# A decoder layer step on one core: one array for x's two parts, three blocks in one first stage, and 512-column matmuls in six index query blocks

## The chip, the cores and the metric

The kernel runs on one core of a Trainium2 chip. The metric is the device time of one execution, in microseconds. Five engines run their own instruction streams and meet at semaphores: TensorE (PE in the profile, with its weight loads as PEld), VectorE (DVE), ScalarE (ACT), GpSimd (POOL) and SyncE (SP), which here issues DMA transfers. Matmul results land in PSUM, everything else lives in SBUF.

## The reference

The reference is one inference step of one decoder layer, in float32, for a prompt of 256 tokens and for 8 requests with 8 new tokens and 2048 cached tokens each. Together these are 320 token columns (`NT`): 256 of the prompt, then 64 of the samples. A prompt query keeps 64 keys, so the first 64 prompt tokens (`SKIP = 64`) keep all they have and need no index query. One input projection makes all heads:

```
z = jnp.einsum('btd,dn->btn', h, w)          # d = 2048
aq, ak, av, ag, iq, ik, iw, bq, bf, bi, bg, mq, mg = jnp.split(z, cuts, axis=-1)
iq = _rope(iq.reshape(n_b, n_t, H_IDX, D_IDX), pos)
sc = jnp.einsum('bth,bthl->btl', iw, jax.nn.relu(dots))   # dots = iq . ik
_, sel = lax.top_k(sc, n_sel)                # keys that each query attends to
```

`aq`, `ak`, `av` are queries, keys and values of a sparse attention with 8 heads of 128; `iq` (16 heads of 64), `ik` and `iw` make the index scores that select the keys. A gated linear recurrence (`bq`, `bf`, `bi`), a cross-attention into memory tokens, gates, an output projection and a layer norm follow. The selection depends on order among scores, so the products are made with nearly full float32 precision.

## The kernel before

All large products use a rounded float32 type (`F32R`) that PE streams at one column per cycle. To keep precision, each operand is split in a high part (a cast) and a low part (the operand less its high part), and three products are summed: weight high times x high, weight high times x low, weight low times x high.

x is held transposed, 16 slices of 128 rows and 320 columns: `xh` and `xl` are two arrays of `[128, 16, 320]`. A block of the projection is 128 output columns: its weights are the stationary operand, 16 slices K of 128x128, and the moving operand is x. So a full block is 16 x 3 matmuls of 320 columns, and an index query block (`iq`, eight of them) 16 x 3 of 256 columns, because it leaves out the first 64 tokens. The sum of a block stands in a PSUM bank of the tag `pj`, of which there are two. Other PSUM tags are `mA`, `mB` (two banks each), `va` and `kv`.

For each block SP loads weights (`wr`), ACT casts them to `wh`, DVE (later in the program DVE or POOL) subtracts to `wl`, in pieces of 512 columns; there are four buffers of `wh` and of `wl`. When a block is done, its `ev_...` function takes it from PSUM: for `iq`, DVE shuffles and multiplies with the rotary tables straight from PSUM, and POOL multiplies and adds.

The order of all instructions is written out when the program is built. A planner (`Plan`) keeps an estimated time for each engine and a ready time for each tile; the loop at the end issues the next piece of matmul work when its operands are ready by that plan, and lets generators in a background list put small jobs on DVE, ACT and POOL between. `wspec` is the list of weight pieces in the order in which PE takes them; `half` counts them, and some thresholds (which engine subtracts, when page loads begin) are numbers of such pieces. On the chip the order is fixed, and only semaphores wait.

The list starts with the index keys (`ikw`, 80 columns: 64 of the key, 16 of the weights) and the query block `iq0`, interleaved two slices at a time; then `iq1` to `iq7`, then the eight `aq` blocks, then the rest (`PROJECTIONS`). The first pieces have loads of their own: x in pairs of slices (`in_xT`, the first two pairs on ACT's queue), the index key weights (`in_wik`) and iq0's weights (`in_wt`) in four parts each. Before that, PE runs 32 matmuls on a zeroed tile (`kv<-t`, bfloat16, 256 columns).

Once index keys and queries exist, `idx_load`, `key_scores` and others compute scores and selection in the background; cached pages stream through (`pg` tiles), and PE alternates between projection blocks and page work. Names of buffers carry a number that tells one use of a tag from the next.

Of the kernel before, what the change touches and what calls it, by code (L numbers as in the profile page):

```python
# [28 lines left out]
SKIP = 64  # L29
HALF = 1032  # L30
PROJECTIONS = ["ikw", "iq", "aq", "ak", "av", "b0", "b1", "g0", "b2", "g1", "b3", "mem", "mq", "g3", "g2"]
# [26 lines left out]
class Plan:  # L58
# [61 lines left out]
    def dma(self, q, out, in_):  # L120
# [15 lines left out]
        self.t["DMA"] = end = max(self.t["DMA"], t, 0.9) + nbytes / (380e3 if t > 7 else 270e3)  # L136
# [91 lines left out]
def hymba_step(ctx: ExitStack, tc: tile.TileContext, I, O):  # L228
# [85 lines left out]
    xh = const([128, 16, NT], "xh", F32R)  # L314
    xl = const([128, 16, NT], "xl", F32R)
# [18 lines left out]
    plan.split |= {early.tensor.name, stacked.tensor.name}  # L334
    plan.skip |= {xh.tensor.name, xl.tensor.name, avS.tensor.name}
# [27 lines left out]
    def ev_iq(i):  # L363
        def f(ps):
            if i == 0:
                st["q"] = new([128, 8, NS], "pg")
            c, s = (t[:, SKIP:] for t in tabi)
            sh, x = T(256), T(256)
            DVE.stream_shuffle(sh, ps[:, SKIP:], sh_idx)
            DVE.tensor_mul(x, ps[:, SKIP:], c)  # L370
            POOL.tensor_mul(sh, sh, s)
            POOL.tensor_add(st["q"][:, i, :], x[:, 256 - SKIP:], sh[:, 256 - SKIP:])
            IQ[i] = T(256 - SKIP)
            POOL.tensor_add(IQ[i], x[:, 0:256 - SKIP], sh[:, 0:256 - SKIP])
            free(x, sh)
            if i == 7:
                free(*tabi)
            done.add(("iq", i))
        return f

# [143 lines left out]
    def add_block(kind, i):  # L524
        nk = 2 if (kind, i) in (("ikw", 0), ("iq", 0)) else 8
        if kind == "ikw":
            add_T(I["wik"], ev_ikw, 80, nk)
# [3 lines left out]
        else:  # L531
            base, ev = {"iq": (32, ev_iq), "aq": (0, ev_aq), "ak": (8, ev_ak), "av": (16, ev_av), "mq": (56, ev_mq),
                        "bf": (44, None), "bq": (40, None), "bi": (48, None), "g": (24, None)}[kind]
            if kind == "g":
                add_T(wt[24 + i if i < 8 else 44 + i if i < 12 else 48 + i], ev_gate(i, i % 4 == 3))
            else:
                add_T(wt[base + i], ev(i) if ev else ev_b((kind, i)), nk=nk, skip=SKIP if kind == "iq" else 0)

    for name in PROJECTIONS:
        if name[0] == "b":  # L540
# [3 lines left out]
        else:  # L544
            todo = [(name, i) for i in range({"ikw": 1, "mem": 1, "mq": 4}.get(name, 8))]
        for kind, i in todo:
            add_block(kind, i)
    wspec[0:16] = [wspec[8 * (i % 2) + i // 2] for i in range(16)]
# [61 lines left out]
    def prep(i, j):  # L610
# [29 lines left out]
        if i < 52:  # L640
# [1002 lines left out]
    def half_ready(i, q):  # L1643
        s = wspec[i]
        if i not in WH:
            return False
        p = part_of(i, q)
# [609 lines left out]
```

## Time and profile before

| | |
|---|---|
| median of 3 runs | 858.19 us (858.04 to 858.48) |
| profiled execution | 858.96 us, of which the span of instructions is 857.2 us |
| granted clock of PE over the span | 0.997 |
| matmuls, as the profile counts them | 6904 |
| data moved by DMA | 266.49 MB, 311 GB/s in the mean |

A line of a group has the engine, the operation, the tile that it writes and those that it reads, partitions by columns, the count, the busy time and the mean time of one. A matmul is shown with the time from its start until its modelled end (0.28 us for 256 columns), but the next one starts long before that, so what a matmul costs is the time from start to start. The profile puts nearly all instructions on one helper line (L156), so tiles and times tell them apart, not lines.

### The profile page before, as it was taken

How to read it: one execution, taken by the hardware profiler on the slowest of the kernel's cores; microseconds unless marked ns; L12 is line 12 of the kernel's file. 1: busy time of each engine (PE TensorE's matmuls, PEld its weight loads, DVE VectorE, ACT ScalarE, POOL GpSimd, SP SyncE). 2: the span in 40 equal slices, each digit the busy share in tenths (PEclk: the TensorE clock that was granted, in tenths of full speed). 3: DMA queues.
4: the chain of work that ended last, by engine and by line, in shares of the span. 5: the costliest groups of instructions: out<-in, count | busy, mean ns of one | idle time of the engine just before them, and what ended most of it. 6: DMA issues, size and time to landing. Idle time of an engine off the chain costs nothing.

```text
span 857.2 us, 19206 instructions
## 1 busy us (share of the span) xinstructions
PE 846.6 (99%) x6904; PEld 719.7 (84%) x6906; DVE 552.4 (64%) x1103; ACT 425.8 (50%) x915; POOL 310.5 (36%) x323
## 2 busy tenths in 40 slices
PE   9999999999999999999999999999999999999996
PEld 8999988889989888878878888777887889888885
DVE  6698999564987985743574547557545343954655
ACT  6555666544445435444454554555445353744432
POOL 0576653256634461220132214333311100724424
PEclk9999999999999999999999999999999999999998
DMA  8765555799999999999999999999999988856633
GB/s 312 217 184 171 177 151 177 277 377 383 411 378 383 357 335 354 382 379 402 386 325 412 408 349 400 403 393 375 345 410 401 337 337 283 281 172 199 194 97 122
DMA packets 84368, 266.49 MB, mean 311 GB/s; under 512 B 10609, under 2 KB 21810, under 8 KB 83634
## 3 DMA queue, kind: packets, MB, share of 16 engines
q1 hardware_dynamic: 82962, 262.52, 83.9%
q0 software_dynamic: 1024, 2.10, 0.8%
q8 instruction: 54, 0.88, 0.4%
q10 hardware_dynamic: 288, 0.66, 0.3%
q14 instruction: 40, 0.33, 0.1%
HBM read 256.50 MB, written 8.73 MB: 309 GB/s over the span
## 4 chain that ended last, share of the span: by engine, by line
PE 98%; DVE 1%; ACT 0%; issue 0%; DVEq 0%
PE pj L156 56%; PE mB L156 12%; PE va L156 10%; PE mA L156 10%; PE kv L156 8%; PE kv L1926 1%; DVE pg L156 0%; DVE t L156 0%; DVE cat L156 0%; DVE wl L156 0%; ACT t L156 0%; ACT wh L156 0%; DVE s L156 0%; DVEq L156 0%; DVEq L2243 0%
## 5 line engine op out<-in xcount | busy, mean ns | idle before, releaser
L156 ACT CAST wh<-wr 128x512 fp32r<-128x512 f32 x338 | 207.3, 619 | 244.2 <-PE pj L156 182.3
L156 PE MATMUL pj<-xh,wh 128*128 128x320 f32 (+1 forms) x1008 | 318.9, 316 | 0.0
L156 PE MATMUL pj<-xh,wl 128*128 128x320 f32 (+1 forms) x1008 | 308.6, 306 | 0.1
L156 PE MATMUL pj<-xl,wh 128*128 128x320 f32 (+1 forms) x1008 | 308.3, 306 | 0.0
L156 DVE TENSOR_TENSOR wl<-wr,wh 128x512 fp32r<-128x512 f32 x236 | 179.5, 767 | 194.4 <-ACT wh L156 177.8
L156 POOL TENSOR_TENSOR wl<-wr,wh 128x512 fp32r<-128x512 f32 x102 | 136.9, 1347 | 243.0 <-ACT wh L156 198.3
L156 PEld LDWEIGHTS pj<-xh,wh 128*128 128x128 f32 x1008 | 189.6, 188 | 18.3 <-issue 15.0
L156 PEld LDWEIGHTS pj<-xl,wh 128*128 128x128 f32 x1008 | 189.8, 188 | 1.3
L156 PEld LDWEIGHTS pj<-xh,wl 128*128 128x128 f32 x1008 | 189.5, 188 | 0.3 <-DVE wl L156 0.3
L156 POOL TENSOR_TENSOR t<-t,t 128x256 f32<-128x256 f32 (+3 forms) x53 | 46.2, 871 | 118.9 <-ACT t L156 54.4
L156 PE MATMUL kv<-pg,qpad 128*32 128x256 f32 (+1 forms) x916 | 59.2, 380 | 0.0
L156 PE MATMUL va<-pg,PT 128*32 128x512 f32 x456 | 58.4, 595 | 0.0
L156 PEld LDWEIGHTS kv<-pg,qpad 128*32 128x32 f32 (+1 forms) x916 | 31.6, 110 | 21.0 <-issue 1.9
L156 PEld LDWEIGHTS va<-pg,PT 128*32 128x32 f32 x456 | 14.6, 109 | 30.4 <-issue 28.1
L156 DVE MAX8 PT<-PT 128x8 f32<-128x1032 f32 x32 | 39.5, 1233 | 0.5
L156 DVE MATCH_REPLACE8 PT<-PT 128x1032 f32<-128x1032 f32 x32 | 39.0, 1218 | 0.0
L156 POOL DMA_INDIRECT S<-in_ci,row x24 | 25.5, 1062 | 25.3 <-DVE row L156 17.3
L156 PE MATMUL mB<-t,wh 128*128 128x256 f32 x128 | 24.4, 289 | 0.0
L156 POOL TENSOR_TENSOR t<-t,tabm 128x320 f32<-128x320 f32 x16 | 14.1, 880 | 28.4 <-DVE t L156 27.8
L156 POOL TENSOR_TENSOR bp<-t,bp 128x128 f32<-128x128 f32 (+1 forms) x17 | 10.5, 620 | 37.0 <-ACT bp L156 37.0
L156 ACT ACTIVATE S<-kv 128x512 f32<-128x512 f32 x16 | 9.6, 597 | 27.7 <-PE kv L156 27.7
L156 PEld LDWEIGHTS mB<-t,wh 128*128 128x128 f32 x128 | 20.7, 191 | 1.2
(384 smaller groups left out, 1339.1 us busy)
## 6 DMA issues: line engine op xcount, KB each, us to landing
wr<-in_wt SPq DMA_DIRECT2D x126, 512.0 KB
pg<-in_ck SPq DMA_DIRECT2D x114, 512.0 KB
pg<-in_cv SPq DMA_DIRECT2D x114, 512.0 KB
wr<-in_wo SPq DMA_DIRECT2D x36, 512.0 KB
wr<-in_wm SPq DMA_DIRECT2D x16, 512.0 KB
S<-in_ck SPq DMA_DIRECT2D x14, 512.0 KB
S<-in_cv SPq DMA_DIRECT2D x14, 512.0 KB
pg<-in_cXV SPq DMA_DIRECT2D x8, 512.0 KB
```

Source lines behind the costliest of these rows:

```text
L156: res = f(*a, **k)
L1926: nc.tensor.matmul(warm_ps, warm[:, 0:128], warm, start=True, stop=True)
```

## The change

1. `xh` and `xl` become two halves of one array `xhl` of `[128, 16, 2, 320]`: for each slice the high part stands beside the low part.
2. The index keys, `iq0` and `iq1` become one first stage of ten pieces (`FIRST = 10`): four of one slice, six of two. A piece is one transfer of x and all three blocks' weights of that slice, from an array `in_first` laid out on the host, 656 columns a slice (320 of x, 80 + 128 + 128 of weights). All ten go through SP's queue. For each piece ACT casts x, ACT (DVE for the first two) casts the weights, and DVE makes both low parts. PE takes all three blocks in turn, into banks of `va`, `mA` and `pj`; the sums are the same.
3. The other six index query blocks are mixed with the `aq` blocks: aq0, iq2, iq3, iq4, aq1, iq5, iq6, aq2, iq7, aq3 to aq7.
4. In these six, the weight's high part is multiplied with x's high and low part in one matmul of 512 columns, into the two halves of a bank; the weight's low part times x's high part adds 256 columns to the first half. ACT copies the second half out and DVE adds the first half, before shuffle and product, which now read SBUF.
5. 18 warm-up matmuls instead of 32; some small loads and the iota on POOL are issued earlier; the thresholds that count pieces go down by eight, as the list has eight fewer pieces ahead of them; the planner's early transfer rate goes from 270 to 350 KB per us.

```diff
-PROJECTIONS = ["ikw", "iq", "aq", "ak", "av", "b0", ...
+PROJECTIONS = ["first", "queries", "ak", "av", "b0", ...
+FIRST = 10
...
-    xh = const([128, 16, NT], "xh", F32R)
-    xl = const([128, 16, NT], "xl", F32R)
+    xhl = const([128, 16, 2, NT], "xhl", F32R)
+    xh, xl = xhl[:, :, 0, :], xhl[:, :, 1, :]
...
+            x = T(256)
+            if i > 1:
+                ACT.copy(x, ps[:, 1, :])
+            plan.pinned.add(ps.tensor.name)
+            bg.insert(0, [rotate_query(i, ps, x), None])
...
+    def rotate_query(i, ps, x):
+        c, s = (t[:, SKIP:] for t in tabi)
+        sh = T(256)
+        if i > 1:
+            yield need(x, ps=0)
+            DVE.tensor_add(x, x, ps[:, 0, :])
+        y = x if i > 1 else ps[:, SKIP:]
+        DVE.stream_shuffle(sh, y, sh_idx)
+        DVE.tensor_mul(x, y, c)
+        plan.pinned.discard(ps.tensor.name)
...
-        if i < 52:
+        if i < 44:
             DVE.tensor_sub(lo[:, 0:w], raw, hi[:, 0:w].bitcast(F32))
...
+    def first_quantum(i):
+        s = wspec[i]
+        if i == 0:
+            s["ps"] = [PS([128, NT], which) for which in ("va", "mA", "pj")]
+        else:
+            s["ps"] = wspec[i - 1]["ps"]
+        h3, l3 = s["w"]
+        for w, x in ((h3, xh), (h3, xl), (l3, xh)):
+            for ps, c, x0 in zip(s["ps"], firsts, (0, SKIP, SKIP)):
+                for j, K in enumerate(s["ks"]):
+                    PE.matmul(ps[0:c.stop - c.start, x0:], w[:, j, c], x[:, K, x0:],
+                              start=K == 0 and w is h3 and x is xh, stop=K == 15 and w is l3)
...
             for j, K in ks:
+                if x0:
+                    PE.matmul(both, h3[:, j, :], xhl[:, K, :, x0:], start=K == 0, stop=K == 15, skip_group_check=True)
+                    PE.matmul(ps, l3[:, j, :], xh[:, K, x0:], start=False, stop=K == 15, skip_group_check=True)
+                    continue
...
+    def prep_first(a):
+        s = wspec[a]
+        t, ks = s["ks"][0] // 2, slice(s["ks"][0], s["ks"][-1] + 1)
+        raw = raws[t][:, first_cols(a, NT + WIDE)].rearrange("p (j c) -> p j c", c=NT + WIDE)
+        hi, lo = (x[t][:, first_cols(a, WIDE)].rearrange("p (j c) -> p j c", c=WIDE) for x in (his, los))
+        ACT.copy(xh[:, ks], raw[:, :, 0:NT])
+        (ACT.copy if a > 1 else DVE.tensor_copy)(hi, raw[:, :, NT:])
+        DVE.tensor_sub(xl[:, ks], raw[:, :, 0:NT], xh[:, ks].bitcast(F32))
+        DVE.tensor_sub(lo, raw[:, :, NT:], hi.bitcast(F32))
...
-    for _ in range(32):
+    for _ in range(18):
         nc.tensor.matmul(warm_ps, warm[:, 0:128], warm, start=True, stop=True)
```

The order moves at the start and in the query blocks. First PE's first real matmuls, right behind the warm-ups. `PT`, `qpad` and `bp` hold high parts of weights there, `cat` and `pg` low parts; `va` is the sum of the index keys, `mA` of iq0, `pj` of iq0 before and iq1 now. Before:

```order
L156 MATMUL va_186<-xh,PT_88 80x320
L156 MATMUL va_186<-xh,cat_4_84 80x320
L156 MATMUL va_186<-xh,PT_88 80x320
L156 MATMUL va_186<-xh,cat_4_84 80x320
L156 MATMUL va_186<-xl,PT_88 80x320 x2
L156 MATMUL pj_193<-xh,qpad_89 128x256
L156 MATMUL pj_193<-xh,pg_90 128x256
L156 MATMUL pj_193<-xh,qpad_89 128x256
L156 MATMUL pj_193<-xh,pg_90 128x256
L156 MATMUL pj_193<-xl,qpad_89 128x256 x2
```

and in the change:

```order
L157 MATMUL va_184<-xhl,PT_93 80x320
L157 MATMUL mA_185<-xhl,PT_93 128x256
L157 MATMUL pj_186<-xhl,PT_93 128x256
L157 MATMUL va_184<-xhl,PT_93 80x320
L157 MATMUL mA_185<-xhl,PT_93 128x256
L157 MATMUL pj_186<-xhl,PT_93 128x256
L157 MATMUL va_184<-xhl,cat_4_83 80x320
L157 MATMUL mA_185<-xhl,cat_4_83 128x256
L157 MATMUL pj_186<-xhl,cat_4_83 128x256
```

Before, two slices at a time go through two blocks; now one slice at a time goes through three blocks, first with the high parts of x and weights, then with x's low part, then with the weights' low part.

Second, PE at the first index scores: `mA<-t,t` are products of index keys and a rotated query. Before, in block iq3:

```order
L156 MATMUL mA_559<-t_325,t_85 128x64
L156 MATMUL mA_561<-ident,t_325 128x16 x2
L156 MATMUL pj_509<-xh,wh_479 128x256
L156 MATMUL pj_509<-xl,wh_479 128x256
L156 MATMUL pj_509<-xh,wl_480 128x256
```

and in the change, right after block aq0, in block iq2:

```order
L157 MATMUL mA_477<-t_356,t_84 128x64
L157 MATMUL mB_479<-ident,t_356 128x16 x2
L157 MATMUL pj_519<-xhl,wh_395 128x512
L157 MATMUL pj_519<-xhl,wl_396 128x256
L157 MATMUL pj_519<-xhl,wh_395 128x512
L157 MATMUL pj_519<-xhl,wl_396 128x256
L157 MATMUL pj_519<-xhl,wh_395 128x512
L157 MATMUL pj_519<-xhl,wl_396 128x256
L157 MATMUL pj_519<-xhl,wh_395 128x512
L157 MATMUL pj_519<-xhl,wl_396 128x256
L157 MATMUL mA_532<-t_355,t_385 128x128
L157 MATMUL mA_533<-t_355,t_385 128x128
```

Twelve matmuls of 256 columns lie between the first two rows and the scores before, of which three are shown; now four of 512 and four of 256 do.

Third, DVE in the same place. Before:

```order
L156 TENSOR_TENSOR wl_533<-wr_404,wh_532 128x512
L156 TENSOR_TENSOR wl_549<-wr_404,wh_548 128x512
L156 CAST row_552<-rows 128x2
L156 TENSOR_TENSOR t_492<-mA_559,csm 128x4x8 x2
L156 TENSOR_TENSOR t_493<-mA_559,csm 128x4x8 x2
L156 TENSOR_SCALAR cat_3_83<-mA_561 128x32
```

and in the change:

```order
L157 TENSOR_TENSOR wl_445<-wr_323,wh_444 128x512
L157 CAST row_448<-rows 128x2
L157 TENSOR_TENSOR wl_471<-wr_323,wh_470 128x512
L157 TENSOR_TENSOR t_414<-mA_477,csm 128x4x8 x2
L157 TENSOR_TENSOR t_415<-mA_477,csm 128x4x8 x2
L157 TENSOR_SCALAR cat_3_82<-mB_479 128x32
L157 STREAM_SHUFFLE t_508<-pj_363 128x320
L157 TENSOR_TENSOR t_509<-pj_363,tabm 128x320
```

A weight subtraction stands right ahead of the five small jobs in both; after them, the change takes block aq0 (`pj_363`) from its bank.

More of the change, by code (lines that the diff above doesn't have):

```diff
@@ L1646, in half_ready @@
             return False
+        if s["kind"] == "first":
+            return max(plan.avail(x) for x in s["w"]) <= plan.now
         p = part_of(i, q)
@@ L1650, in half_ready @@
         if s["kind"] == "T":
-            return s["k0"] or q or sum(e[0] is not ev_ikw for e in pending) < 2 and plan.slot_free("pj", 2) <= plan.now
+            return s["k0"] or q or sum(e[0] not in other_bank for e in pending) < 2 \
+                and plan.slot_free("pj", 2) <= plan.now
         if s["kind"] == "mem":
@@ L1900, in load_first @@
[L1900 to L1920 removed]
+    WIDE = 80 + 128 + 128
@@ new lines, in hymba_step @@
+    firsts = (slice(0, 80), slice(80, 208), slice(208, WIDE))
+    bps = [new([128, 1024], "bp", F32R) for _ in range(2)]
+    raws = [early[:, 0:1312], early[:, 1312:2624]] + [new([128, 1312], tag) for tag in ("S", "S", "S", "pg", "pg", "pg")]
+    tiles = [new([128, 2320], "PT", F32R), new([128, 2048], "qpad", F32R)], [stacked, new([128, 2048], "pg", F32R)]
+    his, los = ([t[:, 2 * WIDE * i:2 * WIDE * i + 2 * WIDE] for t in ts for i in range(3)] for ts in tiles)
+    his += [t[:, 0:2 * WIDE] for t in bps]
@@ new lines, in hymba_step, with first_cols, load_first @@
+    spare_lo = new([128, 2048], "pg", F32R)
+    los += [spare_lo[:, 2 * WIDE * i:2 * WIDE * i + 2 * WIDE] for i in range(2)]
+    plan.split.update(t.tensor.name for t in raws + his + los)
+    def first_cols(a, w):
+        ks = wspec[a]["ks"]
+        return slice(w * (ks[0] % 2), w * (ks[0] % 2 + len(ks)))
+    def load_first(a):
+        t, c = wspec[a]["ks"][0] // 2, first_cols(a, NT + WIDE)
+        SP.dma_start(raws[t][:, c], I["first"][t][:, c])
+    def prep_first(a):
[7 more added lines that the diff above has]
+        DVE.tensor_sub(lo, raw[:, :, NT:], hi.bitcast(F32))
+        s["w"], WR[a], WH[a], WL[a] = (hi, lo), None, [hi], [lo]
@@ L1955, in setup @@
             SP.dma_start(t, I[n])
+        yield from wait("first")
+        st["qpad"] = new([128, 8, 8, 32], "qpad")
         yield need(pidx)
-        pf, dcol = const([128, 64], "rows"), T8()
-        POOL.iota(dcol[:, 0:1], pattern=[[0, 1]], base=0, channel_multiplier=1,
-                  allow_small_or_imprecise_dtypes=True)
-        DVE.tensor_scalar(dcol[64:128, 0:1], dcol[64:128, 0:1], -64.0, None, op0=OP.add)
+        pf = const([128, 64], "rows")
         DVE.tensor_scalar(pf, pidx, 64.0, dcol[:, 0:1], op0=OP.mult, op1=OP.add)
@@ L2064, in loads @@
             n, b = divmod(npg, 2)
-            if half > 46 and n < len(punits) and page_tag(n) and plan.t["DMA"] < plan.now + 4:
+            if half > 38 and n < len(punits) and page_tag(n) and plan.t["DMA"] < plan.now + 4:
                 load_pages(n, b)
@@ L2075, in loads @@
                 continue
-            if half > 40 and plan.t["SP"] <= plan.now:
+            if half > 32 and plan.t["SP"] <= plan.now:
                 numbers_ahead()
```

134 lines of the change are left out of this document (53 added, 81 removed).

## The prediction

> **What bounds the kernel now.** I read the engine totals first, then the chain of work that ended last, then what TensorE (PE) waited for.
>
> ```profile
> PE 846.6 (99%) x6904; PEld 719.7 (84%) x6906; DVE 552.4 (64%) x1103; ACT 425.8 (50%) x915; POOL 310.5 (36%) x323
> PE 98%; DVE 1%; ACT 0%; issue 0%; DVEq 0%
> PE kv L1926 <- DVE t L156: 1.1, 1, 1.1
> PE mA L156 <- DVE cat L156: 0.9, 1, 0.9
> PE mB L156 <- DVE t L156: 0.3, 1, 0.3
> ```
>
> PE is busy 99% of the span and is 98% of the chain. Its three waits (total, times, longest, in us) add up to 2.3 us. So the time is PE's work, plus its start, plus a tail; what the other engines do counts only where they make PE wait. A change is worth what it takes off PE's own stream. Two stretches could break this reading (columns: length, then busy time and count of PE, PEld, DVE, ACT, POOL, then clock, DMA share, GB/s):
>
> ```profile
> 40.00:60.00 20.00, 19.88 (x167) 19.16 (x167) 19.77 (x45) 10.81 (x22) 13.24 (x15) 1.00 0.54 158
> 350.00:690.00 340.00, 339.61 (x3069) 273.25 (x3070) 188.70 (x404) 164.04 (x378) 87.49 (x104) 1.00 1.00 382
> ```
>
> From 40 to 60 us, in the query blocks, VectorE (DVE) is as full as PE. From 350 to 690 us the DMA engines are full beside a full PE. Both return below as rivals.
>
> **The start.** Pieces of the chain (start, length, what, count):
>
> ```profile
> 1.07 5.81 PE kv L1926 x32
> 6.88 0.87 PE va L156 x6
> 10.23 0.88 PE va L156 x6
> 19.07 15.12 PE pj L156 x126
> 120.25 4.39 PE pj L156 x30
> ```
>
> Then the same start on the timeline, the warm-ups in two windows, and the DMA rate microsecond by microsecond:
>
> ```profile
> 4.61 0.46 ACT L156 CAST PT<-S 128x320 fp32r<-128x320 f32 x1 [1.67 <-DMA S<-in_wik]
> 4.97 0.72 ACT L156 CAST xh<-pg 128x640 fp32r<-128x640 f32 x1
> 5.10 0.49 DVE L156 TENSOR_TENSOR cat<-S,PT 128x320 fp32r<-128x320 f32 x1 [4.08 <-ACT PT L156]
> 5.73 0.83 DVE L156 TENSOR_TENSOR xl<-pg,xh 128x640 fp32r<-128x640 f32 x1
> 6.64 0.39 PE L156 MATMUL va<-xh,PT 128*80 128x320 f32 x1
> 1.10:5.00 3.90, 3.90 (x19) 0.00 (x0) 0.00 (x0) 0.00 (x0) 1.00 0.81 227
> 5.20:6.60 1.40, 1.40 (x13) 0.00 (x0) 0.00 (x0) 0.00 (x0) 1.00 1.04 372
> 1.00:2.00 1.00, 0.93 (x5) 0.67 (x6) 0.01 (x1) 0.34 (x1) 0.94 (x5) 1.00 0.61 31
> 2.00:3.00 1.00, 1.00 (x7) 0.67 (x6) 0.00 (x0) 0.94 (x1) 0.00 (x0) 1.00 0.48 119
> 3.00:4.00 1.00, 1.00 (x6) 0.70 (x5) 0.00 (x0) 0.00 (x0) 0.00 (x0) 1.00 1.06 382
> ```
>
> The first operands are cast by 5.7 us, but the first real matmul starts at 6.64 us, when the 32 warm-ups are through: the warm-ups end that wait, not the data. A warm-up takes some 0.21 us in the first window (19 in 3.90 us) and 0.11 us in the second, so the array speeds up near 5.1 us, although the clock column says 1.00 throughout.
>
> **Part 1, shorter start.** The 126 matmuls of the row at 19.07 take 15.12/126 = 0.120 us each (256 columns); the row of 30 gives 4.39/30 = 0.146 us (320 columns). Six of the 126 end block iq0 and 48 are iq1, so before, the index keys, iq0 and iq1 are done at 19.07 + 54 x 0.120 = 25.55 us. The change does just this work in its first stage. Eighteen warm-ups at 0.21 us, the first of them at 1.07 us, end at about 4.9 us. The work is 48 x 0.146 + 96 x 0.120 = 18.53 us, so it would end at 23.43 us without a wait. Waits it will have: the first piece is 128 x 656 x 4 B = 336 KB, and the last three rows above sum to 532 KB by 4.0 us, so its bytes are in near 3.5 us. How long after that the cast can begin: the two first casts now stand at 4.61 and 4.97 us, so I bound it by 4.1 and 4.9 us and take 4.4. Then DVE does three jobs for each of the first two K slices (a 336-column cast that no row shows, bounded by 0.2 and 0.5 us and taken as the 0.49 of the subtraction of 320), two for the next two slices, all about 0.5 us: its ten jobs end at 9.4 us. PE needs 0.146 + 2 x 0.120 = 0.386 us per third of a slice; following the two rows of jobs against each other it finishes the fourth slice at 10.1 us instead of 9.53. From there a pair costs DVE 0.83 + 0.87 and PE 2.32 us, so PE leads. The stage ends near 24.0 us: **gain 1.55 us** (1.05 with the data at 4.9 us, 2.1 with no wait).
>
> **Part 2, the wide matmuls.** In six index blocks of 16 slices, two 256-column matmuls become one of 512.
>
> ```profile
> 760.02 0.39 PE L156 MATMUL mB<-wh,xh 128*128 128x512 f32 x1
> 760.25 0.39 PE L156 MATMUL mB<-wh,xl 128*128 128x512 f32 x1
> 760.47 0.39 PE L156 MATMUL mB<-wl,xh 128*128 128x512 f32 x1
> 760.70 0.39 PE L156 MATMUL pj<-wh,qpad 128*128 128x512 f32 x1
> ```
>
> From start to start three take 0.68 us, 0.227 each, against 2 x 0.120 = 0.240. The columns are the same; only the 0.013 us per instruction falls away: 96 x 0.013 = **1.25 us**. No row has a moving operand in two stretches 64 columns apart, as here; bounds are 0 (it pays as two) and 1.25, and I take the second, since the operand is otherwise that of these rows. The Trainium skill (TensorE: Matmul & The Clock Gate, "Wait — 56ns, not 53.3ns?") gives a fixed cost of about 2.5 ns per warm matmul; by that the saving would be 96 x 0.0025, an estimate of 0.24 us. The rows above show 13 ns, and they decide.
>
> **Part 3, the wait of 0.9 us** on DVE:
>
> ```profile
> 34.95 1.63 PE pj L156 x12
> 35.80 1.10 DVE L156 TENSOR_TENSOR wl<-wr,wh 128x512 fp32r<-128x512 f32 x1 [1.78 <-ACT wh L156]
> 36.90 0.47 DVE L156 TENSOR_TENSOR t<-mA,csm 128x32 f32<-128x32 f32 x4
> 37.29 0.17 DVE L156 TENSOR_SCALAR cat<-mA 128x32 f32<-128x32 f32 x1
> 37.51 0.93 PE mA L156 x8
> ```
>
> PE ran out of its 12 matmuls at 36.59 us; DVE had still to finish a weight subtraction and five small jobs. In the change this place follows block aq0: PE is there at 24.0 + 48 x 0.146 + 0.6 + 4 x (0.227 + 0.120) = 33.0 us. The subtraction ahead of the small jobs needs a cast whose buffer falls free at aq0's end (31.0 us): 0.6 for the cast, 0.7 for the subtraction, 0.64 for the small jobs, 32.95 us. So the wait is met almost exactly: **gain 0.8 us** (bounds 0 and 0.94).
>
> **Part 4, what is added.** Each wide block has two halves to add.
>
> ```profile
> L156 ACT COPY t<-mB 128x256 f32<-128x256 f32 x11 | 3.7, 375 | 3.2 <-PE mB L156 1.8 <-DVE t L156 1.4
> 26.79 0.45 DVE L156 STREAM_SHUFFLE t<-pj 128x256 f32<-128x256 f32 x1
> 27.13 0.41 DVE L156 TENSOR_TENSOR t<-pj,t 128x256 f32<-128x256 f32 x1
> ```
>
> That is 6 x 0.375 us on ScalarE (ACT) and 6 x 0.41 us on DVE. The two PSUM banks hide it: a bank was free after shuffle and product (0.86 us of work), now after copy and sum (0.79), and PE asks for it again a whole block later, 16 x 0.347 = 5.55 us at least. Mixing main query blocks (48 x 0.146 = 7.0 us) among them stretches DVE's work over more PE time. Moved with the blocks are their loads on SP, the threshold for DVE's subtractions and the page loads' thresholds, each shifted by the eight entries that the list lost, so they stand at the same block as before; the indirect gathers on POOL stay behind the same setup. For waits that the new order makes I allow 0.4 us, with bounds 0 and 2.0, about what the waits of the whole kernel are now without the first.
>
> **Sum.** -1.55 - 1.25 - 0.8 + 0.4 = -3.2 us. The profiled execution took 858.96 us (span 857.2), so 855.8 for it; it lies 0.77 over the median of the runs, 858.19, which gives **855.0 us**.
>
> **Rivals.** (1) The wide form pays as two: no gain in part 2, 856.2 us. For it: no row has the shape; against it: the rows at 760 us.
> (2) PE idles between the last warm-up and the first operands, and the array falls back to the slow rate. The first 19 warm-ups needed 4.0 us to leave it; a second such time at half rate costs 2.0 us: 857.0 us. Against it: the gap is at most 0.5 us. The Trainium skill (same page, "Part 1: The HAM clock gate") has the rate set by activity in a free-running window of about 3.4 us; by that rule 18 warm-ups suffice or fail by where the window lies, and no run here shows where.
> (3) The DMA engines bind from 150 to 690 us, and PE waits there for what it won: 858.2 us. For it: the share of 1.00. Against it: none of PE's waits names a DMA.
> (4) Slower: in the query blocks DVE is the bound, and the bank of each wide block comes free late because copy and sum queue behind weight subtractions. With the 0.9 us of part 3 at each of six blocks, 6 x 0.94 = 5.6 us: 855.0 - 0.4 + 5.6 = 860.2 us. It turns the result from 0.53 us per block on (3.2/6). For it: 19.77 of 20 us on DVE. Against it: that stretch loses PE hardly anything today, and it gets looser.
>
> **How the numbers follow.** Forecast 0.61, rivals 0.07, 0.10, 0.10 and 0.12. About 0.2% (1.7 us) is what a measurement can tell. Forecast and (1) lie below 856.5, (2) mostly above: faster 0.70. (2) and (3) are the same: 0.18. (4) is slower: 0.12. Low end: gains 2.1 + 1.25 + 0.94 and no new wait, 853.9, less 0.9 for waits I don't see: 853.0. High end 858.4, which takes in (3). The likeliest case's own range is 853.5 to 856.4.
>
> **What would show it.** First real matmul near 5.0 us and the first stage done near 24 us; a wide and a narrow matmul together 0.347 us; no wait of 0.9 us on DVE before 40 us; PE waits under 1.5 us in all after the start. Wrong it is if the wide form shows 0.24 us, if the matmuls after 5 us run at 0.21 us, or if PE waits for DVE or ACT at the wide blocks.

## The result, and the profile after

The changed kernel is slower. It takes 865.97 us (median of 4 runs, 865.27 to 866.34) against 858.12 us (857.86 to 858.48) for the kernel before, measured in turn: a ratio of 1.0089, 95% interval 1.0077 to 1.0101, or 7.85 us between the medians. The forecast was 855.0 us.

The page of the changed kernel, its engine totals and its chain of work:

```profile
PE 849.5 (98%) x6793; PEld 715.2 (83%) x6796; DVE 557.2 (64%) x1111; ACT 424.6 (49%) x915; POOL 322.8 (37%) x327
PE 95%; DVE 2%; DMA 2%; ACT 1%; issue 0%; POOL 0%; DVEq 0%; SPq 0%; ACTq 0%; POOLq 0%
```

PE's waits in it (total, times, longest, in us):

```profile
PE kv L157 <- DMA pg<-in_ck: 3.0, 2, 2.3
PE pj L157 <- DVE t L157: 1.6, 1, 1.6
PE kv L1963 <- DVE t L157: 1.1, 1, 1.1
```

PE is no longer 98% of the chain but 95%, and a DMA stands in it with 2%. The wait of 0.9 us on "DVE cat" is gone, as forecast. Two new waits have come: 3.0 us for pages of cached keys (`pg<-in_ck`), and 1.6 us on DVE.

The start ended when it was foreseen. The timeline has the first real matmuls, the end of the first stage (the first matmul of aq0 reads `wh`), and five slices of a wide block:

```profile
4.74 0.62 PE L157 MATMUL va<-xhl,PT 128*80 128x320 f32 x1
5.16 0.41 PE L157 MATMUL mA<-xhl,PT 128*128 128x256 f32 x1
5.37 0.42 PE L157 MATMUL pj<-xhl,PT 128*128 128x256 f32 x1
...
6.36 0.28 PE L157 MATMUL mA<-xhl,cat 128*128 128x256 f32 x1
6.47 0.28 PE L157 MATMUL pj<-xhl,cat 128*128 128x256 f32 x1
...
23.80 0.46 PE L157 MATMUL pj<-xhl,wh 128*128 128x320 f32 x2
...
35.97 0.39 PE L157 MATMUL pj<-xhl,wh 128*128 128x512 f32 x1
36.20 0.29 PE L157 MATMUL pj<-xhl,wl 128*128 128x256 f32 x1
...
37.73 0.40 PE L157 MATMUL pj<-xhl,wh 128*128 128x512 f32 x1
```

The first real matmul starts at 4.74 us (forecast "near 5.0"), the first stage ends at 23.80 ("near 24"). A wide and a narrow matmul together take (37.73 - 35.97)/5 = 0.352 us, against 3 x 0.120 before: 8 ns saved a slice, not 13, so 96 x 8 ns = 0.77 us. One sign of a wrong forecast did come: the first matmuls behind 5 us are slow. From `mA` to `pj` it takes 5.37 - 5.16 = 0.21 us, and 6.47 - 6.36 = 0.11 us a little later. Against the later pace, the matmuls from 4.74 to 6.2 us lose about 0.7 us, and the stage ended on time nevertheless.

What was won is lost later. The chain near the first page products and near 208 us (start, length, what, count), then the rows of the timeline in which PE waits there; the bracket has the wait:

```profile
143.45 0.59 ACT cat L157
144.04 0.49 ACT pg L157
...
145.05 0.68 DVE cat L157
...
145.77 0.70 DVE cat L157
146.49 0.33 SPq L157
...
147.02 6.66 DMA pg<-in_ck
...
198.57 3.66 PE kv L157 x64
202.23 0.08 SPq L157
...
202.51 7.94 DMA pg<-in_ck
```

```profile
150.80 2.35 PE L157 MATMUL kv<-pg,qpad 128*32 128x256 f32 x36
153.82 1.92 PE L157 MATMUL kv<-pg,qpad 128*32 128x256 f32 x28 [0.66 <-DMA pg<-in_ck]
...
210.58 0.41 PE L157 MATMUL kv<-pg,qpad 128*32 128x256 f32 x2 [2.31 <-DMA pg<-in_ck]
```

Two windows around the second wait, and one microsecond inside the second (length, then busy time and count of PE, PEld, DVE, ACT, POOL, then clock, DMA share, GB/s):

```profile
200.00:210.00 10.00, 8.27 (x77) 6.13 (x68) 3.55 (x6) 4.20 (x7) 2.56 (x2) 1.00 0.86 314
210.00:220.00 10.00, 7.82 (x61) 5.02 (x62) 4.01 (x10) 0.25 (x1) 2.68 (x4) 0.83 1.01 404
212.00:213.00 1.00, 1.00 (x16) 0.69 (x12) 0.00 (x0) 0.00 (x0) 0.00 (x0) 0.50 1.03 418
```

Near 150 us, index work on ACT and DVE, which reads a buffer of the tag `pg`, holds it until 146.5 us. Only then can SP issue the page's load. It lands at 153.7 us, and PE, which began on that group of pages at 150.8 us, goes on at 153.82. This costs PE a wait of 0.7 us.

Near 208 us the wait is 2.3 us, and what held the load is another thing: the chain goes back from it to PE's own page products, which end at 202.23 us, and not to index work. Behind this wait the granted clock falls. It is 0.50 from 211 to 214 us and 0.83 in the mean from 210 to 220 us, which is 10 x 0.17 x 2 = 3.4 us at half speed. By the Trainium skill (TensorE: Matmul & The Clock Gate, "Part 1: The HAM clock gate") the array falls to half speed after an idle window of about 3.4 us, and comes back after a busy one of about 3.4 us. The length of the stretch agrees with the second figure; the idle time ahead of it, 2.3 us in one piece, is shorter than the first.

Where the 7.0 us between the two profiled executions lie is seen by the same matmul in both: the first product of page values (`va<-pg,PT`) starts at 367.02 us before and at 371.60 after; the first matmul of the output projection at 731.79 and 736.63; the last matmul at 848.92 and 855.94. So 4.6 us are lost by 367 us, on top of what was won at the start, 0.3 more until 731 us, and 2.2 us in the output projection.

### The profile page after: what moved, and what is told of

Its sections match the earlier page's. It is cut to its first block, busy times and chain, and to the rows that moved or that the text cites. A ratio compares the mean times of both kernels' runs of the same rounds, so it can differ in the third digit from the quotient of the medians.

```text
span 864.2 us, 18969 instructions
## 1 busy us (share of the span) xinstructions
PE 849.5 (98%) x6793; PEld 715.2 (83%) x6796; DVE 557.2 (64%) x1111; ACT 424.6 (49%) x915; POOL 322.8 (37%) x327
## 3 DMA queue, kind: packets, MB, share of 16 engines
q0 software_dynamic: 1024, 2.10, 0.8%
## 4 chain that ended last, share of the span: by engine, by line
PE 95%; DVE 2%; DMA 2%; ACT 1%; issue 0%; POOL 0%; DVEq 0%; SPq 0%; ACTq 0%; POOLq 0%
PE pj L157 54%; PE mB L157 12%; PE va L157 10%; PE mA L157 10%; PE kv L157 8%; DMA pg<-in_ck 2%; PE kv L1963 0%; DVE t L157 0%; DVE cat L157 0%; DVE pg L157 0%; DVE wl L157 0%; DVE bp L157 0%; POOL wl L157 0%; ACT t L157 0%; ACT wh L157 0%
## 5 line engine op out<-in xcount | busy, mean ns | idle before, releaser
L157 PE MATMUL pj<-xhl,wh 128*128 128x320 f32 (+1 forms) x1888 | 440.3, 319 | 1.6 <-DVE t L157 1.6
L157 PEld LDWEIGHTS pj<-xhl,wh 128*128 128x128 f32 x1888 | 316.4, 188 | 25.2 <-issue 12.9
L157 PE MATMUL pj<-xhl,wl 128*128 128x320 f32 (+1 forms) x992 | 304.9, 307 | 0.4 <-DVE wl L157 0.3
L157 DVE TENSOR_TENSOR wl<-wr,wh 128x512 fp32r<-128x512 f32 x226 | 172.8, 773 | 183.4 <-ACT wh L157 167.4
L157 POOL TENSOR_TENSOR wl<-wr,wh 128x512 fp32r<-128x512 f32 x108 | 147.6, 1372 | 247.8 <-ACT wh L157 220.8
L157 PEld LDWEIGHTS pj<-xhl,wl 128*128 128x128 f32 x992 | 186.4, 188 | 1.1 <-DVE wl L157 1.0
L157 PE MATMUL mB<-wh,xhl 128*128 128x512 f32 x108 | 34.0, 396 | 0.0
L157 PE MATMUL mA<-wh,xhl 128*128 128x512 f32 x96 | 30.1, 394 | 0.0
L157 PEld LDWEIGHTS mB<-wh,xhl 128*128 128x128 f32 x108 | 20.3, 188 | 4.7
L157 DVE TENSOR_TENSOR cat<-S,cat 64x512 fp32r<-64x512 f32 x24 | 17.4, 724 | 9.2 <-ACT cat L157 8.6
```

The costliest lines, as they stand in the source:

```text
L157: res = f(*a, **k)
```

## The experiments

Times are medians, with the ratio to the kernel before, run in turn on the same chip, and its 95% interval. "The list" is the fixed order on PE that the planner writes; "planned" is the planner's own estimate of a time, which stands in its `Plan` while the program is built and is here a thing under test, not a measure. Edits are shown abridged. The groups ran on different chips, so kernels of different groups are compared by their ratios.

**First: is it the pages, and what slows the output projection?** Four kernels. e1 alters the page rule

```diff
-        if any(... plan.avail(PG[n, b]) > plan.now ...)
+        if any(... plan.avail(PG[n, b]) + 6.0 > plan.now ...)   # first eight units
```

> The change with one rule of its planner altered: PE may take the page work of the first eight K pages only 6 us after the planned landing of their pages. Nothing is left out. Theory A (the loss comes from PE meeting pages that have not landed: in the changed kernel 3.0 us of waits named DMA pg<-in_ck, 2.7 us ahead of the first V page products of the index recurrence at 207.9, 2.2 us at 215.3 behind them, and after the stall 3.4 us at a granted clock of 0.5): the DMA waits go, the granted clock stays 1.00 from 200 to 220 us, and about 5 us come back: 861 us (860 to 862.5), what is left being the slower 512-column matmuls of the output projection. Theory B (the mixed query order and the later index blocks made PE's list itself worse, whatever the pages do): the waits move to another place and the time stays within 1.5 us of the changed kernel's 866.0. Theory C (the clock fell for another reason than the waits): the waits go, some 2.5 us come back (863.5), and the 0.5 row stays.

864.47 us, 1.0072 (1.0055 to 1.0089): nearest to theory B, whose bound of 1.5 us it just misses. The waits on pages shrank to 1.6 us in all, and none is left near 208 us. But a wait of 1.5 us on "DVE cat" is new at 205 us, and right behind it the clock fell for 3.4 us, in an execution that was the slowest of the four (867.04 us). So a wait for DVE will do for the clock as well as one for pages. The planner, told that pages are late, wrote a list of 856.7 us planned length where the changed kernel's has 850.4. A delay in the rule is no cure, and the run does not settle theory A.

e2 joins x's parts in the kernel before; e3 and e4 only move buffers, those of `wh` and `wl` among them:

```diff
-    xh = const([128, 16, NT], "xh", F32R)            # e2, on the kernel before
-    xl = const([128, 16, NT], "xl", F32R)
+    xhl = const([128, 16, 2, NT], "xhl", F32R)
+    xh, xl = xhl[:, :, 0, :], xhl[:, :, 1, :]

+    const([128, 96], "pad")                          # e3, on the kernel before

-    dcol = T8()                                      # e4, on the changed kernel
+    dcol = const([128, 8], "dcol")
```

> The kernel before with one edit: x's two parts lie interleaved in one array, so that the slices that PE loads as stationary operand in the output projection stand 2560 bytes apart instead of 1280. Order of all instructions and all other addresses as before. Theory S (the layout of x's array makes a 512-column matmul cost 232 instead of 227 ns in the output projection): the rows from 738 to 848 us show 231 to 232 ns from start to start, and the time is 858.1 + 2.2 = 860.3 us. Theory M (it is where the moving operand lies, or something that comes after the fall of the clock): 227 ns and 858.1 us, no change within 0.5 us.

> The kernel before with 384 bytes a partition of unused space ahead of the weight buffers, so that the cast weights (moving operand in the output projection) begin at a multiple of 1024 bytes, as they do in the changed kernel, instead of 640 beyond one. Order of all instructions as before. Theory M (where the moving operand lies sets 232 instead of 227 ns for 512 columns): 231 to 232 ns from start to start from 738 to 848 us and 858.1 + 2.2 = 860.3 us. Theory S (x's array) or a cause that comes after the fall of the clock: 227 ns and 858.1 us within 0.5 us.

> The changed kernel with one small tile moved to another place, by which the cast weights begin 736 bytes beyond a multiple of 1024 instead of at one. Order of all instructions as in the changed kernel. Theory M (where the moving operand lies): 227 ns a 512-column matmul from 738 to 848 us and 866.0 - 2.2 = 863.8 us. Theory S (x's array) or a cause that comes after the fall of the clock: 231 to 232 ns and 866.0 us within 0.5 us.

e2: 860.30 us, 1.0025 (1.0015 to 1.0034). e3: 859.81 us, 1.0024 (1.0012 to 1.0035). e4: 867.12 us, 1.0109 (1.0092 to 1.0126). The same 40 us of the output projection, in which nearly all matmuls have 512 columns, as a window; what counts is PE's count, the first one in brackets. First the kernel before:

```profile
765.00:805.00 40.00, 40.00 (x177) 33.02 (x176) 19.99 (x30) 17.36 (x30) 17.25 (x13) 1.00 0.66 203
```

In the changed kernel:

```profile
765.00:805.00 40.00, 40.00 (x175) 32.49 (x174) 21.65 (x32) 18.61 (x32) 17.13 (x13) 1.00 0.65 192
```

In e2:

```profile
765.00:805.00 40.00, 40.00 (x178) 33.00 (x177) 21.61 (x33) 17.50 (x30) 17.18 (x14) 1.00 0.66 194
```

In e3:

```profile
765.00:805.00 40.00, 40.00 (x174) 32.50 (x173) 19.68 (x30) 16.84 (x30) 17.23 (x13) 1.00 0.66 198
```

In e4:

```profile
765.00:805.00 40.00, 40.00 (x173) 32.23 (x172) 22.17 (x33) 17.61 (x31) 18.36 (x14) 1.00 0.62 185
```

With the weights 640 bytes beyond a multiple of 1024 (before, e2) 177 or 178 matmuls fit; at 0 (changed, e3) 174 or 175; at 736 (e4) 173. The clock is 1.00 in every row, and PE never idle. So the slow matmuls go with the place of the weights, as theory M said, with the correction that a multiple of 1024 is not what is bad: 736 is no better, and e4 did not gain. It was 640 that was good; why, these runs don't show. In e3 every buffer behind the pad moved along, so the weights were not moved alone; x, the other operand of most of these matmuls, lies at one and the same address in all the programs.

e2's time of 860.30 us is what theory S had forecast, and by chance: its window shows 178 matmuls, so the layout of x's array does not slow them. Its order is not that of the kernel before either, though the expectation says so: the planner, which keeps one ready time for a tile, wrote another list (the trace has 1102 instructions on DVE and 324 on POOL, before 1103 and 323). In its trace PE waits 1.3 us between 735 and 765 us, 0.5 of it on `xhl`.

e4 shows one more thing. Its profiled execution took 863.61 us, and in it the granted clock never fell; the other three took 866.8 to 868.0 us with a mean clock of 0.995 instead of 0.998. So the half-speed stretch behind the waits comes in some executions and not in others. What it is worth is not settled: these are 3.2 to 4.4 us, but the one execution of the changed kernel with a mean clock of 0.998 took 865.27 us, only 0.7 to 1.1 less than its other three at 0.995.

**Second: which part of the change?** Start, mixing and wide matmuls, taken apart; e8 is the changed kernel with the weights back at 640 bytes, got by putting four tiny tiles into one:

```diff
-            todo = [('aq', 0), ('iq', 2), ('iq', 3), ...          # e5 and e6: old order
+            todo = [('iq', i) for i in range(2, 8)] + [('aq', i) for i in range(8)]

-                    PE.matmul(both, h3[:, j, :], xhl[:, K, :, x0:], ...)   # e5 and e7: three narrow
-                    PE.matmul(ps, l3[:, j, :], xh[:, K, x0:], ...)
+                for w, x in ((h3, xh), (h3, xl), (l3, xh)):
+                    PE.matmul(ps, w[:, j, :], x[:, K, x0:], ...)

+    small = const([128, 8], "small")                 # e8, and all kernels after it
+    ngt, eps = small[:, 0:1], small[:, 2:4]
+    one = small[:, 4:5]
-    dcol = T8()
+    dcol = small[:, 6:8]
```

> The changed kernel with only its new first stage (index keys and two index blocks as one piece, 18 warm-ups, one array of x): query blocks in the old order, three 256-column matmuls a slice. PE's list has its first K page products after 152.4 us of matmul work (before 154.1, changed 142.1). Theory P (PE's list reaches the page products ahead of their pages, and how far depends on the mixing and the wide matmuls): no wait on DMA, granted clock 1.00 throughout; 858.2 - 1.9 (first real matmul) + 1.7 (weights at a multiple of 1024 bytes, as the padded kernel before showed) = 858.0 us (857 to 859.5). Theory Q (any earlier start brings PE to pages that come no earlier): waits on DMA of 2 us or more and 861 to 865 us.

> The changed kernel with the old order of query blocks: six index blocks, then eight main blocks; wide matmuls and the new first stage stay. First K page products after 148.5 us of matmul work. Theory P with mixing as the cause: waits on DMA under 1 us, granted clock 1.00; 858.0 - 0.8 (96 x 8 ns of the wide form) = 857.2 us (856.5 to 859.5). If the wide form is as guilty as the mixing (it too makes PE earlier): waits on DMA of 1 to 3 us, and 860 to 864 us. Theory Q as for the run with the new first stage alone: 861 to 865 us.

> The changed kernel with three 256-column matmuls a slice in the index blocks, evacuated as before; mixed order and new first stage stay. First K page products after 147.8 us of matmul work. Theory P with mixing as the cause: waits on DMA of 2 to 3 us, a stretch at a granted clock of 0.5 behind them, and 866.0 + 0.8 = 866.8 us (864 to 867.5). If the wide form is needed for the loss: no wait on DMA and 858 to 860 us.

> The changed kernel with four tiny tiles put into one, by which the cast weights begin 640 bytes beyond a multiple of 1024, as in the kernel before. Order of all instructions as in the changed kernel. If the place of the moving operand sets the 232 ns: 227 ns a 512-column matmul from 738 to 848 us and 866.0 - 1.8 = 864.2 us. If it is something else in the changed kernel: 231 to 233 ns and 866.0 us within 0.7 us.

e5 (start alone): 859.36 us, 1.0000 (0.9984 to 1.0015). e7 (start and mixing): 858.54 us, 0.9991 (0.9981 to 1.0001). e6 (start and wide): 865.28 us, 1.0073 (1.0049 to 1.0096). e8 (all, weights at 640): 862.14 us, 1.0038 (1.0021 to 1.0056). In this group the kernel before itself scattered more (857.70 to 862.24 us). The kernels with wide matmuls lose, those without don't. In the traces of e5 and e7 the first matmul of the output projection starts 2.8 us earlier than in the trace of before, and the 231 to 232 ns there eat most of that up again. So mixing is not to blame: without the wide form it costs nothing.

The 2.8 us are too much, though, since the profiled execution of the kernel before had a slow start. e3 has the same list, and its output projection starts 0.9 us earlier, at 730.87 us. The 32 warm-ups in e3 and in e2:

```profile
1.07 5.07 PE L1927 MATMUL kv<-t 128*128 128x256 bf16 x32 [1.07 <-DVE t L156]
```

```profile
1.07 6.59 PE L1926 MATMUL kv<-t 128*128 128x256 bf16 x32 [1.07 <-DVE t L156]
```

They begin at the same time in the three executions and take 5.07, 5.81 (before) and 6.59 us, because the matmuls go over from 0.21 to 0.11 us at 4.0, 5.5 and 7.1 us. The first real matmul starts at 5.90, 6.64 and 7.42 us. Against e3 the new start is worth 1.9 us.

In e8 the output projection is back at 227 ns:

```profile
765.00:805.00 40.00, 40.00 (x178) 32.96 (x177) 21.39 (x33) 17.57 (x30) 17.09 (x14) 1.00 0.65 190
```

The time falls by 3.8 us against the changed kernel (4.4 by the ratios), of which 2.2 are the placement; its profiled execution had no half-speed stretch. PE's longest wait is the same in e5 and in e7, and neither has a wait for a DMA:

```profile
PE kv L1955 <- DVE t L157: 1.1, 1, 1.1
```

In e6:

```profile
PE pj L157 <- DVE wl L157: 1.3, 3, 0.7
PE mA L157 <- DVE s L157: 1.1, 1, 1.1
```

In e8:

```profile
PE kv L157 <- DMA pg<-in_ck: 2.4, 1, 2.4
PE pj L157 <- DVE t L157: 1.6, 1, 1.6
```

e6 shows no wait for pages at all, as theory P said for mixing as the cause, but its time is far off that theory's 857.2 us and beyond every range that was given. With six wide blocks on end, PE waits for DVE. So the lists with the wide form lose in two ways, by the place that its blocks have.

**Third: is it the list or the form?** e10 makes a tight list without any wide matmul; e11 and e12 keep the wide matmuls in other lists; e9 is the narrow kernel with the weights at 640.

```diff
-        if any(... plan.avail(PG[n, b]) > plan.now ...)           # e10, on e9
+        if any(... plan.avail(PG[n, b]) - 3.0 > plan.now ...)     # first eight units

-            ... ('iq', 5), ('iq', 6), ('aq', 2), ('iq', 7), ...   # e11, on e8
+            ... ('iq', 5), ('iq', 6), ('iq', 7), ('aq', 2), ...

-PACE = 4.8                                                         # e12, on e8
+PACE = 4.4
+            todo = iq2 iq3 iq4 aq0 iq5 iq6 iq7 aq1 ... aq7
```

> The changed kernel without the wide matmuls, and with the cast weights 640 bytes beyond a multiple of 1024. Theory L (each list of PE is worth its planned length plus what the pages come late, and the place of the weights costs 2 us): no wait on DMA, granted clock 1.00, 227 ns in the output projection, and 858.5 - 1.9 = 856.6 us, against about 858.5 for the kernel before: faster by 0.2 to 0.35%. Rival (the slower run with 232 ns was chance, and the run without the wide form has nothing left to win): 858.5 us within 0.7.

> The kernel of e9_nowide640 (no wide matmuls) with one number of the planner altered: it takes the pages of the first eight K units for landed 3 us earlier than it works out. The planned length of PE's list stays 849.6 us, but PE's first use of the last piece of each of the first four page pairs now stands 1.1, 0.4, 1.4 and 1.8 us behind its planned landing instead of 4.6, 5.8, 4.1 and 8 us (the changed kernel has 3.9, 5.3, 6.2 and 0.4). Theory L: PE waits on DMA there, 2 to 6 us in all, and perhaps a stretch at a clock of 0.5: 859 to 864 us. Rival W (the loss is tied to the wide form itself, its copies and sums, and not to the list): no wait on DMA over 0.5 us and 856.6 us.

> The changed kernel with the weights 640 bytes beyond a multiple of 1024 and two entries of its query order exchanged: the last index block stands ahead of the third main block. Wide matmuls and mixing stay, the planned length of PE's list stays 850.4 us, and PE's first uses of the first four page pairs stand 3.2, 3.2, 5.8 and 8.6 us behind their planned landing. Theory L: no wait on DMA over 0.5 us, granted clock 1.00, and 855.5 to 857.5 us. Rival W: the time of the changed kernel with the weights at 640, 862 us within 1.5.

> The changed kernel with the weights 640 bytes beyond a multiple of 1024, three wide index blocks, one main block, three wide index blocks and the other seven main blocks, and the planner's pace 4.4 instead of 4.8. Planned length of PE's list 848.7 us, the shortest of all lists tried; first uses of the first four page pairs 3.2, 5.4, 6.0 and 10.9 us behind their planned landing. Theory L: no wait on DMA, 227 ns, and 858.2 - (851.5 - 848.7) + 1 for what DVE comes late in three index blocks on end = 855 to 857 us, the best of all. Rival D (index blocks on end make DVE the bound, as in the run without mixing, where PE waited 4 us in all on DVE): 858 to 860 us.

e9: 856.85 us, 0.9989 (0.9980 to 0.9998): the time that theory L gave, but only 0.1% under the kernel before, where 0.2 to 0.35 had been expected. It is the only kernel of all whose interval lies wholly below 1. e10: 861.51 us, 1.0033 (1.0021 to 1.0045), as theory L said: without one wide matmul, a list that meets its pages early loses 4.7 us. Its one wait on a DMA:

```profile
PE kv L157 <- DMA pg<-in_ck: 2.9, 1, 2.9
```

The window and the chain there:

```profile
150.00:160.00 10.00, 7.07 (x74) 4.10 (x74) 8.70 (x24) 3.26 (x7) 4.39 (x4) 0.86 0.66 236
```

```profile
147.09 0.70 DVE wl L157
147.80 0.34 SPq L157
...
149.47 7.74 DMA pg<-in_ck
...
157.25 3.52 PE kv L157 x28
```

PE's side is as in the changed kernel, a wait (2.9 us) and then a clock of 0.86 in the mean, with the planned length of the list unchanged at 849.6 us. What holds the load back differs: here SP first waits for a weight buffer that DVE (`wl`) still reads.

e11: 861.08 us, 1.0032 (1.0020 to 1.0044). Here theory L missed. No wait names a page and the clock stays at 1.00 there, and yet the time is rival W's (862 us within 1.5) and by the ratios no better than e8. Its chain between 88 and 110 us, of which these are some of the longest pieces, lies on DVE almost without a break:

```profile
90.44 1.20 DVE bp L157
...
96.96 1.02 DVE cat L157 x4
...
101.79 1.90 DVE cat L157
...
110.09 0.75 PE mA L157 x2
```

e12: 859.82 us, 1.0024 (1.0014 to 1.0035), in rival D's range (858 to 860), with a page wait of 1.4 us beside the waits on DVE, in spite of the shortest planned list of the group (848.7 us).

**Fourth: the sums, or the matmuls?** f1 and f2 leave list and matmuls and cut the work of copy and sum to 8 of 256 columns, which leaves the low part of x out of the index queries; f3 leaves the list and gives each wide matmul as two; f4 gives the sum to POOL. f3 yields other values than the reference; its time alone is read.

```diff
-                ACT.copy(x, ps[:, 1, :])                            # f1 on e11, f2 on e8
+                ACT.copy(x[:, 0:8], ps[:, 1, 0:8])                  # planned as before
-            DVE.tensor_add(x, x, ps[:, 0, :])
+            DVE.tensor_add(x[:, 0:8], x[:, 0:8], ps[:, 0, 0:8])

-            PE.matmul(both, h3[:, j, :], xhl[:, K, :, x0:], ...)    # f3 on e8, planned as one
+            for a, x in enumerate((xh, xl)):
+                nc.tensor.matmul(both[:, a, :], h3[:, j, :], x[:, K, x0:], ...)

-            DVE.tensor_add(x, x, ps[:, 0, :])                       # f4 on e8, with PACE = 4.4
+            ACT.copy(sh, ps[:, 0, :])
+            POOL.tensor_add(x, x, sh)
```

> The kernel of e11_swap with the same list on every engine, but the copy of the low half on ACT and the sum on DVE behind each of the six wide blocks do 8 of their 256 columns; shuffle and product then read the high half from PSUM. The low part of x is so left out of the index queries. It takes 6 x (0.41 - about 0.1) = 1.8 us of work off DVE and about 1.6 us off ACT in the query blocks. In e11_swap the chain of waits ran on DVE from 88 to 110 us. Theory D (the sums of the wide form make DVE the bound there): the waits of PE between 90 and 112 us shrink by 1.5 to 2 us and the time is 859.2 us (858.5 to 859.8) against 861.1 for e11_swap. Rival N (the wide matmuls themselves, or the list, cost it): 861 us within 0.6.

> The changed kernel with the weights 640 bytes beyond a multiple of 1024, the same list on every engine, and copy and sum of each wide block cut to 8 of 256 columns as in f1_swap_cheap. Theory D carried further (DVE's index work comes later by the sums, the page buffer that it holds comes free later, and PE meets the pages): SP's wait for the freed page buffer near 146 us and PE's wait for pages near 208 us shrink by 1 us or more, and the time is 860 to 861 us against 862.1 (e8_a640). Rival N: the waits on DMA stay 2 to 3 us and the time within 0.7 of 862.1.

> The changed kernel with the weights 640 bytes beyond a multiple of 1024 and the same list on every engine, with each wide matmul given as two of 256 columns into the two halves of the same PSUM bank; copies and sums stay. PE's own work is 96 x 0.008 = 0.8 us longer. Theory L (PE arrives at late pages; what it wins or loses ahead of them goes into or out of the wait): the wait on DMA shrinks by about 0.8 us and the time stays within 0.5 of 862.1 us (e8_a640). Rival G (the wide form's gain is real and adds up): 862.9 us.

> The changed kernel with the weights 640 bytes beyond a multiple of 1024, both halves of a wide block copied from PSUM by ACT and summed by POOL instead of DVE, and the planner's pace 4.4. Planned length of PE's list 848.7 us; first uses of the fourth and fifth page pairs with more room than in the changed kernel, the fifth or sixth pair near 228 us with 0.5. Theory D: without the sums DVE is as free as in the narrow kernel; 848.7 - 851.5 + 858.1 = 855.3 us (854.5 to 857.5), if the page pair near 228 us isn't missed by more than 1 us. Rival P (PE meets the pages near 228 us): a wait on DMA of 2 to 4 us and 858 to 861 us.

f1: 858.96 us, 1.0005 (0.9996 to 1.0014): 0.6 us above the kernel before, where e11 was 3.0 above it. Theory D holds for that list: between 85 and 115 us no wait of PE is left, and the chain there is PE's again:

```profile
87.72 8.12 PE pj L157 x54
...
97.53 5.39 PE pj L157 x36
...
103.84 4.40 PE pj L157 x30
```

f2: 862.30 us, 1.0047 (1.0033 to 1.0060), no faster than e8 (1.0021 to 1.0056). The DMA waits go from 2.4 to 2.0 us only, and SP's wait for the page buffer does not move. In the changed kernel, between 136 and 150 us, and in f2:

```profile
SPq L157 <- DVE cat L157: 4.8, 1, 4.8
```

```profile
SPq L157 <- DVE cat L157: 4.8, 1, 4.8
```

So theory D carried further falls: in this list the sums are not what makes the buffer come late. f3: 862.66 us, 1.0050 (1.0037 to 1.0064): list and sums as in e8, no wide matmul, and a time that can't be told from e8's, whose ten runs spread from 859.89 to 865.88 us. Its waits are nearly e8's:

```profile
PE kv L157 <- DMA pg<-in_ck: 2.7, 2, 2.5
PE pj L157 <- DVE t L157: 1.6, 1, 1.6
```

Theory L had asked for a wait for pages 0.8 us shorter; it did not shrink. In the traces f3's output projection starts 1.3 us behind e8's (735.37 for 734.10 us), of which 0.5 is there by 24 us, ahead of any wide block. That leaves about 0.8 us, rival G's figure (862.9 us): as far as two traces tell, the gain of the wide form is kept to the end. It is small beside the loss.

f2 and f3 together: neither the wide matmuls nor their sums, as work, cost the changed kernel its time. The list that the planner wrote around them does. f4: 864.97 us, 1.0078 (1.0064 to 1.0092), rival P and worse: 4.1 us on pages, 2.2 us in six waits on weights, though its planned length is 848.7 us.

**How late each runs against its own plan.** For each kernel, the start of PE's matmuls in the trace less the planned start, in the median over 10 us from the time given:

| kernel | planned length | 50 | 80 | 110 | 170 | 220 | 360 us |
|---|---|---|---|---|---|---|---|
| before | 851.5 | -0.1 | 1.8 | 1.8 | 2.0 | 1.6 | 1.2 |
| e7 start, mixing | 849.6 | -0.9 | -0.8 | 0.7 | 0.7 | 0.5 | 0.3 |
| changed | 850.4 | -0.8 | 0.3 | 1.8 | 2.9 | 7.3 | 7.0 |
| e8 changed, 640 | 850.4 | -0.8 | 0.1 | 1.7 | 2.1 | 4.8 | 4.5 |
| e10 tight, narrow | 849.6 | -0.3 | -0.2 | 1.3 | 6.1 | 6.6 | 6.3 |
| e6 wide, not mixed | 850.6 | 1.5 | 3.7 | 3.9 | 3.6 | 3.3 | 3.0 |
| e11 swap | 850.4 | -0.2 | 0.7 | 3.8 | 3.4 | 3.2 | 2.7 |
| f1 swap, cheap sums | 850.4 | -0.4 | -0.2 | 1.4 | 1.1 | 0.9 | 0.7 |

All lose some 1.5 us in one place (between 80 and 105 us). Beyond that, the tight lists lose where they meet pages (e10 near 157, changed near 150 and 207 us), the others with wide blocks lose to DVE in the query blocks. And the planned lists differ little, those with the new start by a microsecond at most: the wide form shortens PE's planned work by 0.8 us and lengthens its planned idle time by 1.7 us; the chip shows a wait of this size, 1.6 us on "DVE t", in the changed kernel and in e8.

By the plan, the first use of the page piece near 205 us stands 0.4 us behind its landing in the changed kernel; in e9 no piece used by 360 us has less than 2.4 us. The pages are later than planned in both lists: the load that SP issues at 146.49 us in the changed kernel was planned for 140.3, and in e7 one issued at 148.3 was planned for 144.7. The load that PE meets near 208 us was planned to be issued at 199.3 and to land at 204.7 us; it was issued at 202.5 and landed at 210.5, 5.8 us late, while PE stood only 2.8 us behind its plan there.

## Why the prediction was wrong, point by point

*Part 1, shorter start: right in its end.* First real matmul at 4.74 us, stage done at 23.80 us (forecast near 5.0 and 24.0). *Part 3, the wait of 0.9 us: right*, it is gone. With nothing else in the way the two together moved the output projection 2.8 us forward against the trace of before and 1.9 against that of e3, which has the same list (e5, e7); 1.55 + 0.8 = 2.35 had been forecast. One reading under it was off: the warm-ups of the kernel before go over to 0.11 us at 5.5 us, not near 5.1, and the executions show 4.0 to 7.1 us.

*Part 2, the wide matmuls: the sign right, the size too large:* 0.77 us in place of 1.25, 8 ns a slice in place of 13. The form with two stretches takes about 232 ns in the changed kernel and 233 in e8, where the weights lie at 640, not the 227 of the rows at 760 us.

*Part 4, what is added, is the step that failed.* It allowed 0.4 us for waits that the new order makes (bounds 0 and 2.0) and took the rest of the program for unchanged, with page loads "at the same block as before". They do stand at the same block, but two things did not stay. PE reached its first page products 12.9 us earlier (150.8 for 163.7 us), while the last index work on DVE that reads a page buffer came 22 us later (145.8 for 123.6 us); the order of page work against page loads is made anew by the planner at each edit. In its place the runs showed 6.7 us of waits and what follows them. And the whole program was taken to keep its addresses: the weights moved, and the output projection lost 2.15 us, a term that the sum did not have.

The measured terms, each less the trace of before: start and first wait -2.8 (e5, e7); planned list with the wide form against without it +0.9 (850.43 - 849.56); waits against the plan, 7.0 - 0.3 = +6.7 by 360 us (about 1.0 near 60, 1.1 near 150, 4.6 near 207 us, of which some 1.7 is the half clock: e8, without it, lost 2.9 there); place of the weights +2.15. The sum is +6.95, and the profiled executions differ by 7.02 us at the last matmul. With -1.9 for the start it is 7.85, as the medians have it; that it fits to the last figure is luck.

Two more of the named signs came: PE's waits come to 6.6 us in all against "under 1.5", and DVE holds PE up for 1.0 us near 60 us, among the wide blocks, where the chain lies on DVE from 55 to 63 us.

*Rival 3* was nearest: DMA binds and PE waits there for what it won. It was given 0.10 because "none of PE's waits names a DMA". That row describes one list, with the room that this list happens to leave; it says nothing on the next list. And the rival had only the win to lose (858.2 us); waits cost more than the win, since the clock can fall behind them. *Rival 4* (DVE bound, 860.2 us) is real in e6 and e11, and the changed kernel's mixing keeps it down to the 1.0 us near 60 us. *Rival 2* (the slow rate) came in small at 5 us, where the array had not yet left it (0.7 us), and in earnest at 210 us.

What stays open: why the loads are later than planned, 6.2 us for the one at 146.5 us (3.6 in e7's list) and 5.8 us at its landing for the one that costs most. For the first, the chain shows ACT's index work held behind a weight cast and DVE's behind ACT's, and f2 excludes the sums; the cause in the list was not isolated. No run kept the changed list and gave its page near 205 us more room.

## What to carry to other kernels

Where a planner writes the order, an edit is not the sum of its parts: ask first how much room the order leaves between each load's landing and its first use, and how late the chip runs against the plan there, and put the loss of that room into the range. Undoing parts one at a time (start, mixing, form) and running the same list with other work found in a few runs what the diff could not show. A layout edit moves every buffer behind it, so compare the start-to-start time of the commonest matmul in an untouched stage before looking for reasons in the edited one. And one trace of the kernel before is one execution: a second, of a kernel with the same list, moved the worth of the start from 2.8 to 1.9 us.

## What the hardware showed unexpectedly

A 512-column matmul costs 227 ns or 231 to 233 ns by where its operands lie in SBUF, at a granted clock of 1.00 and a PE that never idles: weights 640 bytes beyond a multiple of 1024 were the fast place, 0 and 736 the slow ones. From the output projection's first matmul to the last of all, the traces lose 2.2 us against before at 0 (changed, e7) and 0.5 us or nothing at 640 (e9, e8), over 480 such matmuls.

A wait of 1.5 (e1), 2.1 (f4), 2.3 (changed) or 2.9 us (e10) in the middle of a busy program was enough to halve the granted clock for about 3.4 us; behind waits of 1.8 (e4) and 2.4 us (e8) it stayed at 1.00.

The time at which the warm-up matmuls go over from 0.21 to 0.11 us differed from execution to execution, 4.0, 5.5 and 7.1 us with the first of them at 1.07 us each time, while the clock column said 1.00. With it the first real matmul moved from 5.90 to 7.42 us.
